# A two-block transformer stack in split fp32: operand parts side by side in one 512-column matmul, and a convolution's first tap on ScalarE

## The chip, the cores and the metric

The kernel runs on one core of a Trainium2 chip. The metric is the device time of one execution in microseconds (us). A profiled execution gives the trace from which all rows below come.

The engines are named as the profile names them: PE (TensorE, matmuls; PEld its weight loads), DVE (VectorE), ACT (ScalarE), POOL (GpSimd), SP (issues the DMAs).

## The reference, cut to what matters

256 tokens of 2048 channels pass through two blocks. The first has two layers; each is a mixer and a gated convolution feed-forward ("ffn"), with RMS norms before and after. The second has two "hybrid" layers that mix four kinds of attention. Nearly all arithmetic is projections `h @ w` of 256 tokens with big fp32 weight matrices. The ffn, where the second edit lies:

```python
def causal_dwconv(x, w, b):          # K = 3 taps
    xp = jnp.pad(x, ((0, 0), (K - 1, 0), (0, 0)))
    y = xp[:, 0:T] * w[0]
    for k in range(1, K):
        y = y + xp[:, k:k + T] * w[k]
    return y + b

def channel_mixer(h, up, conv_w, conv_b, down):
    hid = causal_dwconv(h @ up, conv_w, conv_b)
    gate, val = jnp.split(hid, 2, axis=-1)
    return (jax.nn.gelu(gate, approximate=True) * val) @ down
```

## The kernel before, in words

**Layout.** Activations lie transposed: 128 channels on the partitions, 256 tokens along the free axis, so a "column tile" of a projection is 128 output channels and its result is 128 x 256 in PSUM. A k tile is 128 input channels.

**Split products.** PE multiplies in a rounded form of fp32 (float32r). Each operand is therefore kept as a rounded part and the rest that rounding left: weights as `h` and `l` (L147 on ACT rounds, L148 on DVE subtracts, 128 x 1024 at a time), activations as `xh` and `xl` (`split`, L206 and L207; in class `XS` with the norm's gain, L277 and L278). A product is h·xh + l·xh + h·xl, three matmuls of 256 columns into the same PSUM range: L173, L174 and L177 (L180 where more than two columns are open at once, for then the third products follow together). The two parts of activations lie in separate tiles of eight k tiles each.

**Weight stream.** 899 blocks of 512 KB come by DMA on SP's queue into 5 raw buffers and are split into 4 buffers each of `h` and `l`; 8 weight tiles of 128 x 128 per block, in the order in which the program asks for them.

**projT** computes some columns over all k tiles, then evacuates them with `evac` (a callback). Two columns share a PSUM bank (`pts[ci // 2][:, ci % 2]`), out of the pool `pp` of 4 banks. With `hold` the evacuation is handed back as a function, and `hooks` calls such functions in the middle of the next projection: each stage starts with a held group of five or six columns, then a group with hooks, in which the norm's factor is computed. `projV` (L198 to L200) is the same with tokens and channels exchanged: weights are the moving operand, 512 columns at a time. `out_proj` runs six columns together (none in the ffn), then pairs up to column 13, then columns 14 and 15 singly, for the norm that follows at once. The attention's own products use a second PSUM pool, `pa`, of 4 banks.

**Around it.** In the ffn, `unit(j, ps)` takes a pair of columns (gate and value), multiplies with the norm's factor (L532, the reader of PSUM), applies the three taps (L537, then two L540 for each half), gelu (L543, ACT), the product (L544) and `split`. In the projections of queries and keys the evacuation is `ev_mul` (L395); out_proj's are `Post.evac` (L313 square on ACT, L319 on DVE) and, in the hybrid layers, L1103. In the hybrid layers gated linear attention comes first: six levels of decays (L902 to L907), products (L888) and masked copies (L891), then chunk states and a norm (L863 writes its end); after it in the program stand the four column pairs of diff_q and diff_k. The 2 KB tiles `w2` (8 of them) serve all short-lived values, `a8` (13, of 8 KB) the long ones.

**Order.** The program is unrolled. A scheduler orders each engine's instructions ahead of time: of those whose inputs and buffers are ready it takes the one that stands first in the program, moved by the offsets of `tc.high_priority`: new weight blocks 3000 instructions ahead, evacuations `EVAC` = 100 ahead, L888 250 behind. On the chip each engine then works through its list in order.

Of the kernel before, what the change touches and what calls it, by code (L numbers as in the profile page):

```python
# [10 lines left out]
F32 = mybir.dt.float32  # L11
# [4 lines left out]
OP = mybir.AluOpType  # L16
# [49 lines left out]
def kernel(  # L66
# [20 lines left out]
    wk = ctx.enter_context(tc.tile_pool(name="wk", bufs=8))  # L87
# [73 lines left out]
    def projT(ks, cols, key, xs, evac, hooks={}, hold=False):  # L161
        nb = (len(cols) + 1) // 2
        pts = [pp.tile([P, 2, T], F32, tag="pp", name="pp") for _ in range(nb)]
        for i, k in enumerate(ks):
            if i in hooks:
                hooks[i]()
            xh, xl = xs(k)
            last = i == len(ks) - 1
            cs = []
            for ci, c in enumerate(cols):  # L170
                h, l = blk(key(k, c))
                o = pts[ci // 2][:, ci % 2]
                TE.matmul(o, h, xh, start=(i == 0 and ci % 2 == 0), stop=False, skip_group_check=True)  # L173
                TE.matmul(o, l, xh, start=False, stop=False, skip_group_check=True)  # L174
                cs.append((o, h))
                if len(cols) <= 2:
                    TE.matmul(o, h, xl, start=False, stop=last, skip_group_check=True)  # L177
            if len(cols) > 2:
                for o, h in cs:
                    TE.matmul(o, h, xl, start=False, stop=last, skip_group_check=True)  # L180
        def evacs():
            with tc.high_priority(offset=EVAC):
                for b in range(nb):
                    evac(b, pts[b])

        if hold:
            return evacs
        evacs()

    def projV(ks, key, xs, evac):  # L190
        pts = [pp.tile([P, 512], F32, tag="pp", name="pp") for _ in range(2)]
        for i, k in enumerate(ks):
            xh, xl = xs(k)
# [11 lines left out]
    def split(val, hi, lo):  # L205
        S.activation(out=hi, in_=val, func=AF.Copy)  # L206
        V.tensor_tensor(out=lo, in0=val, in1=hi.bitcast(F32), op=OP.subtract)  # L207

# [4 lines left out]
    def rsqrt(ss, n, width):  # L213
        # 1 / sqrt(y), y = ss / width + eps, from p = 2 sqrt(y) of the table and Heron's step: p / 4y + 1 / p
# [52 lines left out]
    class XS:  # L267
        def __init__(self, gname):
            self.g = gname
            self.h = [a8(F32R) for _ in range(2)]  # L270
            self.l = [a8(F32R) for _ in range(2)]
            self.acc = w2()

        def add(self, k, n=2):
            for j in range(k, k + n):
                hi, lo = self.h[j // 8][:, j % 8], self.l[j // 8][:, j % 8]
                S.activation(out=hi, in_=x_t[:, j], func=AF.Copy, scale=pc(self.g, j))  # L277
                V.scalar_tensor_tensor(out=lo, in0=x_t[:, j], scalar=pc(self.g, j), in1=hi.bitcast(F32),  # L278
                                       op0=OP.mult, op1=OP.subtract)
# [8 lines left out]
        def hooks(self, held):  # L288
            # the norm's short products go between those of the second projection, `held` is the first one's end
# [8 lines left out]
        def __call__(self, k):  # L298
            return self.h[k // 8][:, k % 8], self.l[k // 8][:, k % 8]
# [73 lines left out]
    def pipeline(n, first, second, depth=2):  # L373
        # the second half of each item's work trails its first half by `depth` items
# [24 lines left out]
    def mixer0(xs, post):  # L399
# [76 lines left out]
        ph, pl = a8(F32R), a8(F32R)  # L476
        fo = CST["fix"][0]
        for g in range(4):
# [16 lines left out]
            split(po, ph[:, 2 * g : 2 * g + 2], pl[:, 2 * g : 2 * g + 2])  # L495

        mh, ml = [a8(F32R) for _ in range(2)], [a8(F32R) for _ in range(2)]
# [7 lines left out]
        for g in range(4):  # L505
            def ev_pool(b, ps, g=g):
                t = w2()
                for j in range(2):
                    V.tensor_scalar(out=t[:, j], in0=ps[:, j], scalar1=pc("pool_b", 2 * g + j),
                                    scalar2=pc("pool_s", 2 * g + j), op0=OP.add, op1=OP.mult)  # L510
                split(t, mh[1][:, 2 * g : 2 * g + 2], ml[1][:, 2 * g : 2 * g + 2])
            projT(range(2), [0, 1], lambda k, c, g=g: ("pool_w", 0, g * 256 + k * P, ((c * P, P),)),
                  lambda k, g=g: (ph[:, 2 * g + k], pl[:, 2 * g + k]), ev_pool)

        for h in range(0, 8, 2):
            o = pa.tile([P, 2, T], F32, tag="pa", name="pa")
            for j in range(2):
# [3 lines left out]
            split(o, mh[0][:, h : h + 2], ml[0][:, h : h + 2])  # L521
        sqrt_ready(ml[0][:, 7, 0:1].bitcast(F32))
        out_proj(lambda k, c: ("ab_w_out", 0, k * P, ((c * P, P),)), list(range(8, 16)) + list(range(8)),
                 lambda k: (mh[k // 8][:, k % 8], ml[k // 8][:, k % 8]), post.evac, mid=post.mid)

# [1 line left out]
    def ffn(l, xs, post):  # L527
        fh, fl = [a8(F32R) for _ in range(4)], [a8(F32R) for _ in range(4)]

        def unit(j, ps):  # L530
# [14 lines left out]
            split(g[:, 1], fh[j // 8][:, j % 8], fl[j // 8][:, j % 8])  # L545
# [6 lines left out]
        sqrt_ready(fl[3][:, 7, 0:1].bitcast(F32))  # L552
        kd = lambda k, c: ("ffn_down", l, k * P, ((c * P, P),))
        out_proj(kd, range(32), lambda k: (fh[k // 8][:, k % 8], fl[k // 8][:, k % 8]), post.evac, wide=0, mid=post.mid)

# [1 line left out]
    def mixer1(xs, post):  # L557
# [7 lines left out]
        xch, xcl = a8(F32R), a8(F32R)  # L565
# [5 lines left out]
        def rec_conv(j):  # L571
# [5 lines left out]
            split(xc[:, j : j + 2], xch[:, j : j + 2], xcl[:, j : j + 2])  # L577
# [9 lines left out]
        ch, cl = a8(F32R), a8(F32R)  # L587
        for i in range(6):
            g = pc("qng", i) if i < 4 else pc("kvg", i - 4)
            S.activation(out=ch[:, i], in_=z[:, i], func=AF.Copy, scale=g)  # L590
            V.scalar_tensor_tensor(out=cl[:, i], in0=z[:, i], scalar=g, in1=ch[:, i].bitcast(F32),
                                   op0=OP.mult, op1=OP.subtract)
# [5 lines left out]
        # rotary tables  # L598
# [30 lines left out]
        # recurrence gates  # L629
        gr, gi = a8(), a8()  # L630

        def rec_gate(n):
            def ev_g(b, ps):
# [3 lines left out]
                  lambda k: (xch[:, k], xcl[:, k]), ev_g)  # L637
# [3 lines left out]
        # latent projections  # L641
        xq = lambda k: (ch[:, k], cl[:, k])
        xk = lambda k: (ch[:, 4 + k], cl[:, 4 + k])
# [29 lines left out]
        # softplus(-lambda), with log1p(e) = 2 atanh(e / (2 + e))  # L673
# [18 lines left out]
        mh, ml = [a8(F32R), None], [a8(F32R), None]  # L692
# [13 lines left out]
        def values(hh, p):  # L706
# [5 lines left out]
            if hh % 2:  # L712
                split(ob[0], mh[0][:, hh - 1 : hh + 1], ml[0][:, hh - 1 : hh + 1])
# [3 lines left out]
        # output gate  # L717
# [12 lines left out]
        # recurrence  # L730
        mh[1], ml[1] = a8(F32R), a8(F32R)
# [22 lines left out]
        for j in range(0, 8, 2):  # L754
# [3 lines left out]
            split(t, mh[1][:, e], ml[1][:, e])  # L758
        sqrt_ready(ml[1][:, 7, 0:1].bitcast(F32))
        out_proj(lambda k, c: ("cd_w_out", 0, k * P, ((c * P, P),)), list(range(16)), lambda k: (mh[k // 8][:, k % 8], ml[k // 8][:, k % 8]), post.evac,  # L760
                 mid=post.mid)

# [1 line left out]
    def hybrid(l, xs, consts, nxt, mid=None):  # L764
# [14 lines left out]
        # gla q, k, decay and forget-gate logits  # L779
# [25 lines left out]
        # decay logits of gla, forget gates  # L805
# [12 lines left out]
        # log sigmoid  # L818
# [27 lines left out]
        def norm_trans(ob, n2, g, dst):  # L846
            # ob: psum [P tokens, 2 heads, 2 tiles, 128]; dst: [P, 2 heads, T]
# [17 lines left out]
        # ---- gated linear attention  # L865
# [28 lines left out]
        # A level takes the pairs that its halves part, with decays from the first half's last token, and the  # L894
        # diagonal at that token; the diagonal of a chunk's last token rides in a column that the last level spares.
# [20 lines left out]
        # chunk states  # L916
# [48 lines left out]
        # ---- differential attention  # L965
# [65 lines left out]
        # ---- output gates: K tiles fox 0-3, diff 4-7, moba 8-11, gla 12-15  # L1031
        mh, ml = [a8(F32R) for _ in range(2)], [a8(F32R) for _ in range(2)]

        def gate(nm, j):
# [3 lines left out]
            def ev_gate(b, ps):  # L1038
# [6 lines left out]
                split(t, mh[k0 // 8][:, e], ml[k0 // 8][:, e])  # L1045
# [3 lines left out]
        # ---- forgetting and block attention  # L1049
# [56 lines left out]
        sqrt_ready(ml[1][:, 7, 0:1].bitcast(F32))  # L1106
        out_proj(ko, list(range(8)) + list(range(12, 16)) + list(range(8, 12)), lambda k: (mh[k // 8][:, k % 8], ml[k // 8][:, k % 8]), ev_out, mid=mid)

# [210 lines left out]
```

## Time and profile before

| | |
|---|---|
| time, median of 3 runs (lowest to highest) | 2792.28 us (2791.45 to 2794.66) |
| the profiled execution: span from the first to the last instruction | 2789.4 us |
| PE busy | 2754.7 us, 99% |
| DVE busy | 1864.3 us, 67% |
| ACT busy | 1301.3 us, 47% |
| DMA, mean | 174 GB/s, 484.05 MB |
| mean granted PE clock | 0.993 |

A profiled execution lists no time of its own beside its span; the median of the runs is 2.9 us above it. "Busy" is the time in which an engine has at least one instruction under way. Matmuls are pipelined: the length shown of one is longer than the step from its start to the next one's start, so a busy PE says that it doesn't wait, and the step says what a matmul costs.

### The profile page before, as it was taken

How to read it: one execution, taken by the hardware profiler on the slowest of the kernel's cores; microseconds unless marked ns; L12 is line 12 of the kernel's file. 1: busy time of each engine (PE TensorE's matmuls, PEld its weight loads, DVE VectorE, ACT ScalarE, POOL GpSimd, SP SyncE). 2: the span in 40 equal slices, each digit the busy share in tenths (PEclk: the TensorE clock that was granted, in tenths of full speed). 3: DMA queues.
4: the chain of work that ended last, by engine and by line, in shares of the span. 5: the costliest groups of instructions: out<-in, count | busy, mean ns of one | idle time of the engine just before them, and what ended most of it. 6: DMA issues, size and time to landing. Idle time of an engine off the chain costs nothing.

```text
span 2789.4 us, 52130 instructions
## 1 busy us (share of the span) xinstructions
PE 2754.7 (99%) x21738; PEld 2676.3 (96%) x21738; DVE 1864.3 (67%) x2965; ACT 1301.3 (47%) x1749; POOL 5.8 (0%) x10
## 2 busy tenths in 40 slices
PE   9999999999999999999999999999999999999998
PEld 9998999999999998999999999998889999888998
DVE  6776578777644787678777754676756566675655
ACT  5444454444433475454444443454535444453543
POOL 0000000000000000000000000000000000000000
PEclk9999999999999999999999999999999999999999
DMA  7445545555555454545555555554444555444453
GB/s 253 167 159 175 186 156 185 184 182 183 184 186 182 159 173 132 185 159 182 182 183 184 184 183 181 179 177 157 159 155 167 182 182 175 150 158 156 167 182 129
DMA packets 133324, 484.05 MB, mean 174 GB/s; under 512 B 15136, under 2 KB 16224, under 8 KB 132576
## 3 DMA queue, kind: packets, MB, share of 16 engines
q1 hardware_dynamic: 133088, 480.73, 49.8%
q8 instruction: 170, 2.79, 0.4%
q14 instruction: 66, 0.54, 0.1%
HBM read 476.73 MB, written 2.10 MB: 172 GB/s over the span
## 4 chain that ended last, share of the span: by engine, by line
PE 98%; DVE 1%; ACT 0%; issue 0%; DMA 0%; DVEq 0%; ACTq 0%; SPq 0%
PE pp L173 28%; PE pp L174 28%; PE pp L177 24%; PE pp L180 4%; PE pp L200 3%; PE pp L199 3%; PE pp L198 3%; PE pa L386 1%; PE pa L390 1%; PE pn L240 0%; PE pa L1071 0%; PE pa L888 0%; PE pa L1002 0%; PE pn L254 0%; PE pa L1074 0%
## 5 line engine op out<-in xcount | busy, mean ns | idle before, releaser
L173 PE MATMUL pp<-a,h 128*128 128x256 f32 x6528 | 1826.6, 285 | 12.3 <-ACT a L277 6.9
L174 PE MATMUL pp<-a,l 128*128 128x256 f32 x6528 | 1824.5, 284 | 0.0
L148 DVE TENSOR_TENSOR l<-raw,h 128x1024 fp32r<-128x1024 f32 (+1 forms) x900 | 1100.0, 1223 | 804.7 <-ACT h L147 803.6
L177 PE MATMUL pp<-a,h 128*128 128x256 f32 x5600 | 1588.1, 284 | 0.0
L147 ACT ACTIVATE h<-raw 128x1024 fp32r<-128x1024 f32 (+1 forms) x900 | 950.8, 1057 | 1201.3 <-PE pp L177 837.9
L173 PEld LDWEIGHTS pp<-a,h 128*128 128x128 f32 x6528 | 1258.8, 193 | 15.8 <-ACT a L277 7.7
L174 PEld LDWEIGHTS pp<-a,l 128*128 128x128 f32 x6528 | 1258.5, 193 | 2.6 <-issue 0.7
L177 PEld LDWEIGHTS pp<-a,h 128*128 128x128 f32 x5600 | 1074.6, 192 | 2.8 <-issue 1.7
L180 PE MATMUL pp<-a,h 128*128 128x256 f32 x928 | 140.8, 287 | 0.0
L199 PE MATMUL pp<-l,a 128*128 128x512 f32 x328 | 128.3, 391 | 0.0
L198 PE MATMUL pp<-h,a 128*128 128x512 f32 x328 | 128.3, 391 | 0.0
L200 PE MATMUL pp<-h,a 128*128 128x512 f32 x328 | 128.3, 391 | 0.0
L180 PEld LDWEIGHTS pp<-a,h 128*128 128x128 f32 x928 | 126.3, 197 | 0.0
L540 DVE SCALAR_TENSOR_TENSOR w<-w,prm_t,w 128x254 f32<-128x254 f32 (+1 forms) x256 | 116.6, 479 | 2.0
L200 PEld LDWEIGHTS pp<-h,a 128*128 128x128 f32 x328 | 61.6, 188 | 13.4 <-issue 0.7
L199 PEld LDWEIGHTS pp<-l,a 128*128 128x128 f32 x328 | 61.6, 188 | 12.5
L198 PEld LDWEIGHTS pp<-h,a 128*128 128x128 f32 x328 | 61.8, 188 | 12.2
L543 ACT ACTIVATE w<-w 128x256 f32<-128x256 f32 x64 | 26.6, 416 | 89.1 <-DVE w L540 89.1
L364 ACT ACTIVATE w<-w,s 128x128 f32<-128x128 f32 x96 | 42.9, 447 | 52.6 <-DVE s L360 52.6
L206 ACT ACTIVATE a<-w 128x256 fp32r<-128x256 f32 (+1 forms) x92 | 43.7, 477 | 11.5 <-DVE w L544 3.0
L537 DVE TENSOR_SCALAR w<-w,prm_t 128x256 f32<-128x256 f32 x128 | 47.2, 410 | 2.0
L207 DVE TENSOR_TENSOR a<-w,a 128x256 fp32r<-128x256 f32 (+1 forms) x92 | 45.8, 500 | 1.4 <-ACT a L206 1.4
(247 smaller groups left out, 1297.5 us busy)
## 6 DMA issues: line engine op xcount, KB each, us to landing
raw<-in_wpk_dram SPq DMA_DIRECT2D x898, 512.0 KB, 3.3
a<-in_cst_dram SPq DMA_DIRECT2D x2, 1024.0 KB, 5.6
x_t<-in_xT_dram SPq DMA_DIRECT2D x1, 1024.0 KB, 11.2
a<-a SPq DMA_DIRECT2D x8, 128.0 KB, 4.9
out_dram<-a SPq DMA_DIRECT2D x2, 512.0 KB, 2.7
x_t<-in_xT_dram SPq DMA_DIRECT2D x1, 640.0 KB
a<-a SPq DMA_DIRECT2D x8, 64.0 KB
out_dram<-a SPq DMA_DIRECT2D x2, 256.0 KB
```

Source lines behind the costliest of these rows:

```text
L147: S.activation(out=h[:, a], in_=r[:, a], func=AF.Copy)
L148: V.tensor_tensor(out=l[:, a], in0=r[:, a], in1=h[:, a].bitcast(F32), op=OP.subtract)
L173: TE.matmul(o, h, xh, start=(i == 0 and ci % 2 == 0), stop=False, skip_group_check=True)
L174: TE.matmul(o, l, xh, start=False, stop=False, skip_group_check=True)
L177: TE.matmul(o, h, xl, start=False, stop=last, skip_group_check=True)
L180: TE.matmul(o, h, xl, start=False, stop=last, skip_group_check=True)
L198: TE.matmul(pts[q], xh[:, sl], h, start=(i == 0), stop=False, skip_group_check=True)
L199: TE.matmul(pts[q], xh[:, sl], l, start=False, stop=False, skip_group_check=True)
L200: TE.matmul(pts[q], xl[:, sl], h, start=False, stop=last, skip_group_check=True)
L207: V.tensor_tensor(out=lo, in0=val, in1=hi.bitcast(F32), op=OP.subtract)
L537: V.tensor_scalar(out=y[:, s], in0=hp[:, s], scalar1=wc(2), scalar2=pc(f"fcb{l}", c), op0=OP.mult, op1=OP.add)
L540: V.scalar_tensor_tensor(out=y[:, s, d:], in0=hp[:, s, : T - d], scalar=wc(k), in1=y[:, s, d:], op0=OP.mult, op1=OP.add)
```

## The change: what it does

- Activations' two parts lie side by side, in tiles `[P, 4, 2, T]` (class `HL`; four k tiles a tile, k tile by k tile first the rounded part, then the rest). The number of `a8` tiles stays.
- In `projT`, a group is *wide* when it has more than four k tiles, at most two columns, and neither `hold` nor `hooks`; in `out_proj` the pairs are wide and columns 14 and 15 are not. A wide group gives each column a PSUM bank of its own. One matmul takes h times both parts (512 columns, the whole bank), a second l times the rounded part (256 columns, the bank's first half).
- At a wide group's end `summed` adds the halves: per column an ACT copy of the second half to SBUF and a DVE add of the first half to it. `evac` then gets the sum in SBUF in place of PSUM.
- The ffn's first tap (scale and bias) moves from DVE to ACT (`Identity`).
- `w2` has 10 tiles in place of 8. Everything else of the diff puts the new class where the pairs of tiles were; comments go.

```diff
-    wk = ctx.enter_context(tc.tile_pool(name="wk", bufs=8))
+    wk = ctx.enter_context(tc.tile_pool(name="wk", bufs=10))
-    def projT(ks, cols, key, xs, evac, hooks={}, hold=False):
-        nb = (len(cols) + 1) // 2
-        pts = [pp.tile([P, 2, T], F32, tag="pp", name="pp") for _ in range(nb)]
+    def projT(ks, cols, key, xs, evac, hooks={}, hold=False, wide=None):
+        n = len(cols)
+        if wide is None:
+            wide = len(ks) > 4 and n <= 2 and not hold and not hooks
+        pts = [pp.tile([P, 2, T], F32, tag="pp", name="pp") for _ in range(n if wide else (n + 1) // 2)]
...
                 h, l = blk(key(k, c))
+                if wide:
+                    TE.matmul(pts[ci], h, x, start=first, stop=False, skip_group_check=True)
+                    TE.matmul(pts[ci][:, 0], l, x[:, 0], start=False, stop=last, skip_group_check=True)
+                    continue
...
+        def summed():
+            rest, u = w2(), w2()
+            for j in range(n):
+                S.activation(out=rest[:, j], in_=pts[j][:, 1], func=AF.Copy)
+                V.tensor_tensor(out=u[:, j], in0=pts[j][:, 0], in1=rest[:, j], op=OP.add)
+            return u
+
         def evacs():
             with tc.high_priority(offset=EVAC):
-                for b in range(nb):
-                    evac(b, pts[b])
+                if wide:
+                    evac(0, summed())
+                else:
+                    for b in range((n + 1) // 2):
+                        evac(b, pts[b])
...
+    class HL:
+        def __init__(self, n):
+            self.t = [a8(F32R, [P, 4, 2, T]) for _ in range((n + 3) // 4)]
+        def part(self, s, k, n):
+            assert k % 4 + n <= 4
+            return self.t[k // 4][:, k % 4 : k % 4 + n, s]
+        def split(self, val, k, n):
+            hi, lo = self.part(0, k, n), self.part(1, k, n)
+            S.activation(out=hi, in_=val, func=AF.Copy)
+            V.tensor_tensor(out=lo, in0=val, in1=hi.bitcast(F32), op=OP.subtract)
...
+        def __call__(self, k):
+            return self.t[k // 4][:, k % 4]
...
             projT(korder, [c, c + 1] if c < 14 else [c], key, xs, lambda b, ps, c=c: evac(c, ps),
-                  {len(korder) // 2: mid} if mid and c == 15 else {})
+                  {len(korder) // 2: mid} if mid and c == 15 else {}, wide=c < 14)
...
-                V.tensor_scalar(out=y[:, s], in0=hp[:, s], scalar1=wc(2), scalar2=pc(f"fcb{l}", c),
-                                op0=OP.mult, op1=OP.add)
+                S.activation(out=y[:, s], in_=hp[:, s], func=AF.Identity, scale=wc(2), bias=pc(f"fcb{l}", c))
```

## Rows read from the trace of the kernel before

**Rows 1.** The profile's page: span, busy time of PE, its chain by engine.
```profile
span 2789.4 us, 52130 instructions
...
PE 2754.7 (99%) x21738; PEld 2676.3 (96%) x21738; DVE 1864.3 (67%) x2965; ACT 1301.3 (47%) x1749; POOL 5.8 (0%) x10
...
PE 98%; DVE 1%; ACT 0%; issue 0%; DMA 0%; DVEq 0%; ACTq 0%; SPq 0%
```

**Rows 2.** Groups by line: count, busy us, mean ns, idle before and its releasers.
```profile
L177 PE MATMUL pp<-a,h 128*128 128x256 f32 x5600 | 1588.1, 284 | 0.0
...
L180 PE MATMUL pp<-a,h 128*128 128x256 f32 x928 | 140.8, 287 | 0.0
```

**Rows 3.** Timeline of PE, steady stretch: start us, length us, instruction.
```profile
1000.00 0.28 PE L173 MATMUL pp<-a,h 128*128 128x256 f32 x1
...
1005.88 0.28 PE L174 MATMUL pp<-a,l 128*128 128x256 f32 x1
```

**Rows 4.** Timeline of PE in projV.
```profile
239.66 0.39 PE L200 MATMUL pp<-h,a 128*128 128x512 f32 x1
...
242.83 0.39 PE L199 MATMUL pp<-l,a 128*128 128x512 f32 x1
```

**Rows 5.** Windows: length, busy us of PE, PEld, DVE, ACT, POOL; clock, DMA.
```profile
418.50:729.50 311.00, 311.00 (x2594) 311.00 (x2593) 237.90 (x373) 137.14 (x169) 0.00 (x0) 1.00 0.53 183
...
741.10:902.00 160.90, 160.90 (x1344) 160.90 (x1343) 79.90 (x82) 64.88 (x66) 0.00 (x0) 1.00 0.54 183
...
360.00:385.00 25.00, 21.29 (x157) 20.73 (x156) 19.31 (x40) 11.02 (x19) 0.00 (x0) 0.86 0.33 116
```

**Rows 6.** Waits: who waited for whom, us in total, times, longest.
```profile
ACT h L147 <- PE pp L177: 837.9, 512, 4.2
```

**Rows 7.** Groups by line and shape, for ACT and DVE.
```profile
L537 DVE TENSOR_SCALAR w<-w,prm_t 128x256 f32<-128x256 f32 x128 | 47.2, 410 | 2.0
...
L319 DVE TENSOR_SCALAR a<-pp,prm_t 128x256 f32<-128x256 f32 x64 | 30.1, 478 | 0.0
...
L573 ACT ACTIVATE a<-a,prm_t 128x256 f32<-128x256 f32 x8 | 4.4, 589 | 0.0
L634 ACT ACTIVATE a<-pp,prm_t 128x256 f32<-128x256 f32 x8 | 3.8, 477 | 0.0
```

**Rows 8.** Timelines of DVE and PE at the first ffn's start.
```profile
419.60 0.68 DVE L532 TENSOR_TENSOR w<-pp,rb 128x512 f32<-128x512 f32 x1
...
431.25 0.68 DVE L532 TENSOR_TENSOR w<-pp,rb 128x512 f32<-128x512 f32 x1
...
418.51 0.28 PE L173 MATMUL pp<-a,h 128*128 128x256 f32 x1
```

**Rows 9.** Timelines of PE and DVE behind out_proj's six columns.
```profile
305.15 0.28 PE L173 MATMUL pp<-a,h 128*128 128x256 f32 x1
...
307.10 1.27 DVE L319 TENSOR_SCALAR a<-pp,prm_t 128x256 f32<-128x256 f32 x3
...
2226.34 1.29 DVE L1103 TENSOR_TENSOR x_t<-x_t,pp 128x512 f32<-128x512 f32 x2 [1.52 <-PE pp L180]
```

**Rows 10.** Timeline of DVE in the first hybrid layer's gated linear attention.
```profile
1889.13 1.36 DVE L891 COPY_PREDICATED a<-a,pa 128x512 f32<-128x512 uint8 x2
...
1910.08 0.68 DVE L395 TENSOR_TENSOR a<-pp,rb 128x512 f32<-128x512 f32 x1
...
1923.94 0.68 DVE L395 TENSOR_TENSOR a<-pp,rb 128x512 f32<-128x512 f32 x1
```

**Rows 11.** Timeline of PE there.
```profile
1858.00 0.28 PE L173 MATMUL pp<-a,h 128*128 128x256 f32 x1
...
1872.74 1.16 PE L888 MATMUL pa<-w,w 64*128 64x128 f32 x14
```

**Rows 12.** Windows of that stretch, pp's instructions alone, then all.
```profile
1869.40:1910.00 40.60, 25.84 (x189) 23.25 (x188) 0.00 (x0) 0.00 (x0) 1.00 0.32 115
...
1869.40:1910.00 40.60, 39.87 (x357) 35.55 (x356) 30.70 (x58) 14.28 (x29) 0.00 (x0) 1.00 0.32 115
```

More of the change, by code (lines that the diff above doesn't have):

```diff
@@ L166, in projT @@
                 hooks[i]()
-            xh, xl = xs(k)
-            last = i == len(ks) - 1
+            x = xs(k)
+            first, last = i == 0, i == len(ks) - 1
             cs = []
@@ L203, in projV, with scaled, end @@
                 evac(q, pts[q])
-    def split(val, hi, lo):
-        S.activation(out=hi, in_=val, func=AF.Copy)
-        V.tensor_tensor(out=lo, in0=val, in1=hi.bitcast(F32), op=OP.subtract)
+    class HL:
[8 more added lines that the diff above has]
+            V.tensor_tensor(out=lo, in0=val, in1=hi.bitcast(F32), op=OP.subtract)
+        def scaled(self, val, g, k):
+            hi, lo = self.part(0, k, 1)[:, 0], self.part(1, k, 1)[:, 0]
+            S.activation(out=hi, in_=val, func=AF.Copy, scale=g)
+            V.scalar_tensor_tensor(out=lo, in0=val, scalar=g, in1=hi.bitcast(F32), op0=OP.mult, op1=OP.subtract)
+        def end(self, k):
+            return self.part(1, k, 1)[:, 0, 0:1].bitcast(F32)
+        def __call__(self, k):
+            return self.t[k // 4][:, k % 4]
     eps_t = cp.tile([P, 1], F32, name="eps_t")
@@ L269, in __init__ @@
             self.g = gname
-            self.h = [a8(F32R) for _ in range(2)]
-            self.l = [a8(F32R) for _ in range(2)]
+            self.x = HL(KT)
             self.acc = w2()
@@ L275, in add @@
             for j in range(k, k + n):
[L276 to L279, printed above, removed]
+                self.x.scaled(x_t[:, j], pc(self.g, j), j)
         def squares(self):
@@ L494, in mixer0 @@
                                        op0=OP.mult, op1=OP.subtract)
-            split(po, ph[:, 2 * g : 2 * g + 2], pl[:, 2 * g : 2 * g + 2])
-        mh, ml = [a8(F32R) for _ in range(2)], [a8(F32R) for _ in range(2)]
+            po_x.split(po, 2 * g, 2)
+        mx = HL(16)
         vt = a8(shape=[P, 2, 1024])
@@ L520, in mixer0 @@
                      o[:, j], j == 0)
-            split(o, mh[0][:, h : h + 2], ml[0][:, h : h + 2])
-        sqrt_ready(ml[0][:, 7, 0:1].bitcast(F32))
+            mx.split(o, h, 2)
+        sqrt_ready(mx.end(7))
         out_proj(lambda k, c: ("ab_w_out", 0, k * P, ((c * P, P),)), list(range(8, 16)) + list(range(8)),
-                 lambda k: (mh[k // 8][:, k % 8], ml[k // 8][:, k % 8]), post.evac, mid=post.mid)
+                 mx, post.evac, mid=post.mid)
     def ffn(l, xs, post):
-        fh, fl = [a8(F32R) for _ in range(4)], [a8(F32R) for _ in range(4)]
+        fx = HL(32)
         def unit(j, ps):
@@ L551, in ffn @@
             projT(range(KT), gc(j, 1), key, xs, lambda b, ps, j=j: unit(j, ps), xs.hooks(held) if j == 3 else {})
-        sqrt_ready(fl[3][:, 7, 0:1].bitcast(F32))
+        sqrt_ready(fx.end(31))
         kd = lambda k, c: ("ffn_down", l, k * P, ((c * P, P),))
-        out_proj(kd, range(32), lambda k: (fh[k // 8][:, k % 8], fl[k // 8][:, k % 8]), post.evac, wide=0, mid=post.mid)
+        out_proj(kd, range(32), fx, post.evac, wide=0, mid=post.mid)
     def mixer1(xs, post):
@@ L586, in mixer1 @@
         _, rqb = rstd_sb([sqs[i][:, j] for i in range(2) for j in range(2)], 512)
-        ch, cl = a8(F32R), a8(F32R)
+        cx = HL(6)
         for i in range(6):
[L589 to L592, printed above, removed]
+            cx.scaled(z[:, i], pc("qng", i) if i < 4 else pc("kvg", i - 4), i)
         rec_input(2)
@@ L757, in mixer1 @@
             V.tensor_tensor(out=t, in0=gy[:, e], in1=xc[:, e], op=OP.mult)
-            split(t, mh[1][:, e], ml[1][:, e])
-        sqrt_ready(ml[1][:, 7, 0:1].bitcast(F32))
-        out_proj(lambda k, c: ("cd_w_out", 0, k * P, ((c * P, P),)), list(range(16)), lambda k: (mh[k // 8][:, k % 8], ml[k // 8][:, k % 8]), post.evac,
+            mr.split(t, j, 2)
+        sqrt_ready(mr.end(7))
+        out_proj(lambda k, c: ("cd_w_out", 0, k * P, ((c * P, P),)), list(range(16)), lambda k: mx(k) if k < 8 else mr(k - 8), post.evac,
                  mid=post.mid)
@@ L1029, in hybrid @@
         pipeline(4, dscores, dvalues, depth=1)
-        mh, ml = [a8(F32R) for _ in range(2)], [a8(F32R) for _ in range(2)]
+        mx = HL(16)
         def gate(nm, j):
@@ L1104, in ev_out @@
             nxt(c, n)
-        sqrt_ready(ml[1][:, 7, 0:1].bitcast(F32))
-        out_proj(ko, list(range(8)) + list(range(12, 16)) + list(range(8, 12)), lambda k: (mh[k // 8][:, k % 8], ml[k // 8][:, k % 8]), ev_out, mid=mid)
+        sqrt_ready(mx.end(15))
+        out_proj(ko, list(range(8)) + list(range(12, 16)) + list(range(8, 12)), mx, ev_out, mid=mid)
     def dump():
```

43 lines of the change are left out of this document (22 added, 21 removed).

## The prediction, made before the changed kernel was run

> **What bounds the kernel now.** I read the page's busy shares and its chain first [rows 1]: TensorE is busy 2754.7 of 2789.4 us and holds 98% of the chain, so only what changes TensorE's stream, or makes it wait, moves the time. Then the groups by line [rows 2]: the weight-by-operand products are single 256-column matmuls, three for each pair of one k tile and one column tile (I call such a pair a unit): weight part h times operand part h, weight l times operand h, weight h times operand l. L177 is the third product where at most two columns run side by side (5600 units), L180 the third where five or six do (928). Then TensorE's timeline in the steady part [rows 3]: a matmul starts every 0.120 us (49 of them from 1000.00 to 1005.88), although each is shown as 0.28 us long, so the start-to-start step is the price and a unit costs 0.360 us. The same kernel has 512-column matmuls in projV, each with its own weight load as well [rows 4]: 14 steps from 239.66 to 242.83, which is 0.2264 us each. The granted clock is 1.00 in the steady stretches [rows 5], the 2.4 GHz level. Going from 256 to 512 columns costs 0.1064 us, which is 256 columns at 2.4 GHz (0.1067); so of the 0.120 us some 0.0135 us are spent per matmul whatever its width. That is what the change can win, once per unit.
>
> Around TensorE there is room: in the 311 us of the first ffn's up projection DVE is busy 237.9 and ACT 137.1, in its down projection 79.9 and 64.9 of 160.9 [rows 5]. The weight splits run ahead: what ends ACT's longest wait is TensorE giving back weight tiles (837.9 us in 512 waits) [rows 6].
>
> **The change, part by part.**
>
> *The gain.* A wide unit is one 512-column matmul (h times both operand parts) and one of 256 (l times the rounded part): 0.2264 + 0.120 = 0.3464 us in place of 0.360, 0.0136 us less. By the code, wide is every projT with more than four k tiles, one or two columns, no hold and no hooks, and in out_proj every pair before column 14. Counted: layer 0's mixer 528 units, the two ffns 1344 each (28 up pairs of 32 units, 7 down pairs of 64), layer 1's mixer 368, the two hybrid layers 736 each; 5056 in all. They fit L177's 5600 less 192 (with hooks), 96 (one, two or four k tiles) and 256 (columns 14 and 15) [rows 2]. Gain: 5056 x 0.0136 = 68.6 us. Bounds: with the step of 512 columns taken as 0.227 it is 65.7 us; I see no row by which it would be more than 69.
>
> The Trainium skill ("TensorE: Matmul & The Clock Gate", Back-to-back issue gap) speaks against this: it gives the isolated gap as columns over 2.4 GHz plus only 2.5 ns. By that rule a unit would win 2.5 ns, 12.6 us in all. The trace's 0.120 and 0.2264 us do not agree with it.
>
> *What the column's end costs.* 145 wide groups have 288 columns. Each column gets an ACT copy of 256 columns out of PSUM (0.477 us, the nearest row is L634) and a DVE add with one PSUM operand (0.478, L319) [rows 7]; the operation that follows then reads SBUF and not PSUM. That is 137 us more on ACT and 138 on DVE over the kernel. The 128 first taps leave DVE (0.410 each, L537: 52 us) and join ACT (0.589 by the convolution that is there already, L573: 75 us) [rows 7]. In the up projection a unit pair of 11.5 us had 237.9 x 11.52 / 311 = 8.8 us of DVE and 5.1 of ACT [rows 5]; afterwards it lasts 11.1 us with 8.8 + 0.96 - 0.82 = 8.9 and 5.1 + 0.95 + 1.18 = 7.2. Both stay below 11.1, so I price this at nothing; the cover is TensorE's next group. The cover fails if DVE takes 25% longer than that (11.1 / 8.9); each us beyond is then paid in each of the 54 wide pairs of the two up projections. A hand-over between ACT and DVE is added in both places; that is latency of one or two us and not load.
>
> *What is late next: PSUM.* pp has four banks. A group used one, and now uses two, so TensorE may be one group ahead of the evacuation and no longer three. In the steady part that is enough: 11.1 us to do copy, add, copy, add. It is not where an evacuation comes late. I looked for these places:
>
> (a) Ffn start. The six held columns fill three banks, the hooked group the fourth; the next group takes its second column into the bank that L532 reads at 419.60 to 420.28, and would want it at 418.51 + 0.35 [rows 8]. 1.4 us, twice: 3 us (0 to 8, if the fourth bank, read at 431.25, is missed as well).
>
> (b) out_proj's first pair after the six columns. It starts at 305.15, its second column 0.35 later; the first bank of the six is read until two L319 of the three that start at 307.10 are done, 307.95 [rows 9]. 2.4 us in each of two mixers: 5 us. The hybrid layers free that bank with one add of 0.65 us (L1103 [rows 9]): nothing. Where a wide pair stands ahead of the six columns (three places), the third bank is late by some 0.7 us: 2 us.
>
> (c) Gated linear attention in the hybrid layers. The first pair of diff_q is done at 1869.5 (96 matmuls from 1858.00), and its evacuation runs at 1910.08, the first of four L395 for the four pairs; two more follow within 3 us, the last at 1923.94 [rows 10, 11]. Until then three groups sit in PSUM, one bank each, and TensorE works on: 189 of its 357 matmuls between 1869.4 and 1910.0 are for pp [rows 12], 22.7 us at 0.120, so 17.9 us are the attention's. With two banks a group, the third pair can't begin until the first pair's sums are read. That three run at once suggests that they stood for their common output tile and not for DVE; no row says it. The new sums go into w2 tiles, so they can go earlier; but they need two of ten w2 tiles, which the six levels take first. The levels give tiles back as their masked copies are done; the fifth is at 1889.13 [rows 10]. TensorE would be through the second pair at about 1883 (1858.0 + 2 x 11.1 + three levels of 1.2 us [rows 11]): 7 us idle in each layer, 14 in all. Bounds: 0, if the tiles come at once; 25 a layer, if the sums wait for the end of the phase (40.6 - 11.1 - 17.9 = 11.6, and up to 11 for levels that are put behind the second pair, and some more).
>
> Sum: 2789.4 - 68.6 + 3 + 5 + 2 + 14 = 2744.8 us of span. The three runs' median of 2792.28 is 2.9 above the span, so 2748 us. The norm chains and both last columns keep their form, so nothing is taken off there.
>
> **The rivals.**
>
> *Nothing is late.* The list of ready work puts the sums in between, and only 5 us of (a) to (c) are left: 2726 + 2.9 = 2729. For it: DVE has idle time in the phase of (c), 30.7 of 40.6 us busy [rows 12]. Against it: the levels are earlier in the program.
>
> *The sums wait until the attention's end.* 20 us a layer and 10 elsewhere: 2789.4 - 68.6 + 50 + 2.9 = 2774. For it: the evacuations of before ran at the phase's end.
>
> *Slower: PSUM shuts TensorE out.* One mechanism, at (c): if the first pair's banks are held until the last of the evacuations of before (1923.94 [rows 10]), TensorE idles 1923.9 - 1869.5 - 11.1 - 17.9 = 25.4 us, 8 more as the levels' matmuls start behind the second pair, and the clock falls as it does behind a norm, where a stretch of 25 us has 0.86, 3.5 us lost [rows 5]: 37 us a layer. 74 + 10 - 68.6 = +15: 2808. It decides from 29 us a layer. Against it: the sums don't need what the evacuations waited for.
>
> *A cost in each group.* If the weight splits, in order behind copies that wait for a group's end, come late by 0.45 us in every wide group, 65 us go and the time stays at 2790. Against it: weights are four tiles ahead, and ACT waits for TensorE, not the other way [rows 6].
>
> *The 0.0135 us are not per matmul* but come with each 256 columns of an operand tile: a unit stays at 0.360, nothing is won, and with the 24 lost it is 2789.4 + 24 + 2.9 = 2816. The two timelines speak against it [rows 3, 4]. The Trainium skill's rule above is the milder form of it: 12.6 us won would leave 2804.
>
> *The change doesn't do what it says* can't be here: which groups are wide follows from their arguments.
>
> **How the numbers follow.** Forecast (2737 to 2762) 0.55; nothing late 0.13; sums at the phase's end 0.17; shut out 0.07; a cost in each group 0.06; fixed cost not per matmul 0.02. From 2728 to 2782 are 0.83 of it. A measurement of this kernel tells 0.2% (5.6 us) from no change. Faster: the first three and some of the group cost, 0.87; same 0.04; slower 0.09.
>
> **What would show it.** TensorE's timeline in the up projection has steps of 0.226 and 0.120 in turn, 11.1 us a pair: otherwise the gain falls. The 512-column group of projT has 5056 matmuls. DVE's share there stays near 80%, ACT's near 65%, without table loads at each tap. TensorE's waits name the new copy or add, above all 1880 to 1920 us from the start and the like half a thousand later; if they add up to over 30 us, (c) was too cheap, and if they are under 6, too dear. The prediction is wrong if the steady pairs take over 11.2 us, or if a phase that isn't listed waits over 10 us.

## The result, and the profile after

The changed kernel takes 2818.64 us (median of 4 runs, 2810.94 to 2825.84) against 2791.86 (2791.03 to 2794.66) in the runs of the kernel before beside it: ratio 1.0092, 95% interval 1.0066 to 1.0118. The forecast of 2748 was wrong, in sign too. The four runs stand in two places, 2811 (twice) and 2826 (twice); the profiled one is of the first. Its page, which answers to [rows 1]:

```profile
span 2809.2 us, 42670 instructions
...
PE 2728.4 (97%) x16682; PEld 2419.7 (86%) x16682; DVE 1919.1 (68%) x3125; ACT 1465.1 (52%) x2165; POOL 5.8 (0%) x10
...
PEclk9999999999999999999999999979899998889999
```

TensorE has 5056 matmuls fewer and 26 us less busy time, but the span grew by 20. Its granted clock (the line of 40 slices, in tenths of full speed) falls in a few slices, where the kernel before had 9 throughout. To see where the time goes, I took from both traces the start of each projection group on TensorE. The table has before's start and, for each other kernel, how much earlier (-) or later the same group starts. The last four columns are experiments told of below: "narrow d" is run 1, "own" run 3, "order" run 9, "own+order" run 8.

```
first matmul of                before   after  narrow d    own   order  own+order
first ffn, first wide pair      418.5    -6.4     -5.1    -5.6    -5.4     -5.4
first ffn, down projection      741.1   -18.3    -11.0   -11.6   -15.5    -15.5
layer 1's mixer                 931.4   -24.2    -13.5   -14.5   -20.3    -20.3
second ffn, first wide pair    1277.7   -25.8    -14.2   -17.8   -23.3    -24.0
second ffn, down projection    1600.3   -31.7    -20.2   -23.7   -33.4    -34.2
hybrid 0, diff_q/k pair 0      1858.0   -35.9    -23.6   -27.9   -38.5    -40.7
hybrid 0, diff_v               1922.9   -14.5    -23.4   -27.6   -17.9    -40.7
hybrid 0, fox_q pair 2         1944.7   -14.5    -23.4   -27.5   -18.0    -40.6
hybrid 0, moba_q pair 0        2012.7    -2.0     -9.7   -29.4    -6.0    -42.7
hybrid 1, diff_q/k pair 0      2348.9    -7.8    -14.7   -34.5   -11.5    -48.2
hybrid 1, diff_v               2413.9    13.5    -14.4   -34.1     9.4    -48.1
hybrid 1, moba_q pair 0        2503.6    26.0     -2.1   -36.0    21.5    -50.1
last column                    2769.3    20.3     -7.0   -39.5    16.0    -55.3
```

The gain comes, 35.9 us up to the hybrid layers. Each hybrid layer then loses at two places and no other: 21.4 us between the first diff pair and diff_v, 12.5 between fox_q pair 2 and moba_q.

TensorE's timeline in the first ffn (start, length) answers to [rows 3]: the starts are 0.230 and 0.117 us apart, 0.347 a unit.

```profile
599.75 0.39 PE L177 MATMUL pp<-a,h 128*128 128x512 f32 x1
599.98 0.28 PE L178 MATMUL pp<-a,l 128*128 128x256 f32 x1
600.10 0.39 PE L177 MATMUL pp<-a,h 128*128 128x512 f32 x1
600.33 0.28 PE L178 MATMUL pp<-a,l 128*128 128x256 f32 x1
600.45 0.39 PE L177 MATMUL pp<-a,h 128*128 128x512 f32 x1
```

In the second ffn the same instructions run in another pattern, which repeats every three units:

```profile
1400.01 0.40 PE L177 MATMUL pp<-a,h 128*128 128x512 f32 x1
1400.25 0.28 PE L178 MATMUL pp<-a,l 128*128 128x256 f32 x1
1400.36 0.40 PE L177 MATMUL pp<-a,h 128*128 128x512 f32 x1
...
1400.71 0.40 PE L177 MATMUL pp<-a,h 128*128 128x512 f32 x1
...
1401.07 0.40 PE L177 MATMUL pp<-a,h 128*128 128x512 f32 x1
```

From 1400.01 to 1401.07 are three units, so 0.353 us each; this ffn keeps it to the end of its down projection, and the first ffn keeps 0.347. Below, 0.353 is called the slower pattern. The windows (columns as in [rows 5]: length, busy us of PE, PEld, DVE, ACT, POOL, clock, DMA) show both at full clock, and the two stretches that lose:

```profile
411.00:711.00 300.00, 300.00 (x1735) 264.57 (x1735) 237.80 (x368) 183.32 (x280) 0.00 (x0) 1.00 0.57 190
...
1251.90:1568.50 316.60, 316.60 (x1794) 274.37 (x1793) 245.66 (x379) 188.84 (x290) 0.00 (x0) 1.00 0.57 186
...
1848.40:1883.80 35.40, 20.07 (x142) 15.50 (x140) 20.52 (x57) 9.04 (x29) 0.00 (x0) 0.59 0.06 19
1969.40:1986.30 16.90, 9.24 (x35) 5.77 (x33) 9.35 (x37) 8.89 (x27) 0.00 (x0) 0.64 0.12 42
```

At 1848.4 the second diff pair is done; the third starts at 1883.81. In between TensorE has only the attention's 142 matmuls, is idle for 15 us, and runs at a granted clock of 0.59. Timelines of that end, ACT first:

```profile
1869.31 0.28 ACT L886 ACTIVATE w<-pa 128x128 f32<-128x128 f32 x1 [9.48 <-PE pa L994]
...
1878.32 0.28 ACT L886 ACTIVATE w<-pa 128x128 f32<-128x128 f32 x1 [6.26 <-PE pa L994]
...
1879.50 0.30 ACT L260 ACTIVATE nr<-s,eps_t 128x4 f32<-128x4 f32 x1
1879.71 0.91 ACT L193 ACTIVATE w<-pp 128x256 f32<-128x256 f32 x3
```

```profile
1883.34 1.08 DVE L194 TENSOR_TENSOR w<-pp,w 128x256 f32<-128x256 f32 x3
1884.33 0.68 DVE L433 TENSOR_TENSOR a<-w,rb 128x512 f32<-128x512 f32 x1
```

```profile
1880.79 1.25 PE L896 MATMUL pa<-cst_t,w 128*128 128x128 f32 x4 [2.50 <-DVE w L891]
1883.81 0.80 PE L177 MATMUL pp<-a,h 128*128 128x512 f32 x1 [1.76 <-DVE w L194]
```

The copies (L193) of the first pair, whose last matmul started at 1833.33, run 46 us later, right behind the squares (L886) and the root (L260) of the attention's second norm, although ACT stood idle for 9.48 and 6.26 us before. The second place has the same shape: the last matmul of fox_k pair 4 starts at 1954.51, its copies come at 1984.72 behind the norm of the differential attention, and fox_v starts at 1986.30.

```profile
1982.05 0.28 ACT L886 ACTIVATE w<-pa 128x128 f32<-128x128 f32 x1 [4.84 <-PE pa L1058]
...
1984.72 1.19 ACT L193 ACTIVATE w<-pp 128x256 f32<-128x256 f32 x4
```

### The profile page after: what moved, and what is told of

Same layout as the page of the kernel before. It is cut to its first block, busy times and chain, and to the rows that moved or that the text cites. A ratio compares the mean times of both kernels' runs of the same rounds, so it can differ in the third digit from the quotient of the medians.

```text
span 2809.2 us, 42670 instructions
## 1 busy us (share of the span) xinstructions
PE 2728.4 (97%) x16682; PEld 2419.7 (86%) x16682; DVE 1919.1 (68%) x3125; ACT 1465.1 (52%) x2165; POOL 5.8 (0%) x10
## 4 chain that ended last, share of the span: by engine, by line
PE 61%; DVE 2%; ACT 1%; issue 0%; DVEq 0%; ACTq 0%
PE pp L177 25%; PE pp L178 13%; PE pp L181 4%; PE pp L182 4%; PE pp L188 2%; PE pp L218 2%; PE pp L220 2%; PE pp L219 2%; PE pp L185 1%; PE pa L424 0%; PE pa L1105 0%; PE pa L428 0%; DVE a L925 0%; PE pa L896 0%; ACT L260 0%
## 5 line engine op out<-in xcount | busy, mean ns | idle before, releaser
L177 PE MATMUL pp<-a,h 128*128 128x512 f32 x5056 | 1777.6, 396 | 3.5 <-DVE w L194 3.5
L177 PEld LDWEIGHTS pp<-a,h 128*128 128x128 f32 x5056 | 949.9, 188 | 223.3 <-DVE w L194 4.1
L178 PEld LDWEIGHTS pp<-a,l 128*128 128x128 f32 x5056 | 957.7, 189 | 2.7 <-issue 1.0
L181 PE MATMUL pp<-a,h 128*128 128x256 f32 x1472 | 392.2, 288 | 15.2 <-ACT a L242 6.9
L181 PEld LDWEIGHTS pp<-a,h 128*128 128x128 f32 x1472 | 287.3, 195 | 17.3 <-ACT a L242 7.8
L182 PEld LDWEIGHTS pp<-a,l 128*128 128x128 f32 x1472 | 287.2, 195 | 0.6 <-DVE l L148 0.4
L185 PE MATMUL pp<-a,h 128*128 128x256 f32 x544 | 153.9, 283 | 0.0
L188 PE MATMUL pp<-a,h 128*128 128x256 f32 x928 | 140.6, 286 | 0.0
L188 PEld LDWEIGHTS pp<-a,h 128*128 128x128 f32 x928 | 125.8, 196 | 0.0
L193 ACT ACTIVATE w<-pp 128x256 f32<-128x256 f32 x288 | 104.0, 385 | 12.1 <-PE pp L178 0.5
L194 DVE TENSOR_TENSOR w<-pp,w 128x256 f32<-128x256 f32 x288 | 108.4, 417 | 0.0
L577 DVE SCALAR_TENSOR_TENSOR w<-w,prm_t,w 128x255 f32<-128x255 f32 (+1 forms) x256 | 107.4, 479 | 0.2
L185 PEld LDWEIGHTS pp<-a,h 128*128 128x128 f32 x544 | 104.2, 192 | 0.0
L220 PEld LDWEIGHTS pp<-h,a 128*128 128x128 f32 x328 | 62.6, 191 | 13.9 <-issue 1.1
```

Of the source, the lines that this page charges most:

```text
L177: TE.matmul(pts[ci], h, x, start=first, stop=False, skip_group_check=True)
L178: TE.matmul(pts[ci][:, 0], l, x[:, 0], start=False, stop=last, skip_group_check=True)
L181: TE.matmul(o, h, x[:, 0], start=(first and ci % 2 == 0), stop=False, skip_group_check=True)
L182: TE.matmul(o, l, x[:, 0], start=False, stop=False, skip_group_check=True)
L185: TE.matmul(o, h, x[:, 1], start=False, stop=last, skip_group_check=True)
L188: TE.matmul(o, h, x[:, 1], start=False, stop=last, skip_group_check=True)
```

## The experiments

The theory: (1) two unsummed wide groups fill the four banks and shut TensorE out; (2) the sums come late because their buffers are taken from the common ring of work tiles, which are given out in program order, and the norms' tiles are earlier in the program. Rivals: the wide groups' ends load ACT and DVE everywhere; two banks a group are too few whenever the sums come; the sums' priority; the ring's length; the tap. All ratios are to the kernel before, with 95% intervals. A gap is the time from the start of a pair's last matmul to the start of the next projection's first.

**1. Narrow diff pairs.**

```diff
-                      lambda b, ps, o=4 * i + j: ev_mul(dq, xs)(o // 2, ps))
+                      lambda b, ps, o=4 * i + j: ev_mul(dq, xs)(o // 2, ps), wide=False)
```

> Only the four diff_q/diff_k pairs of each hybrid layer go back to three 256-column matmuls in one bank; all else as in the changed kernel. Theory A (two late-summed groups fill the four banks, the third pair shuts TensorE out): from the start of the first pair to the start of diff_v the stretch goes back from 86.3 to about 65 us a layer, so about 2 x 21 us less and some 2 us of lost gain: 2771 us (2785 where the run falls with the upper of the two clusters of the changed kernel, 2811 and 2825). The second place (fox_k 6 to fox_v, 12 us a layer) stays. Theory B (the ends of the wide pairs load ScalarE and VectorE everywhere, the stall at the third pair is only where it shows): the time stays at 2811 to 2825, the stall moves to diff_v.

Measured: 2784.57 us, 0.9976 (0.9966 to 0.9985). The first place is gone (-23.6 to -23.4 in the table), the second stays (13.7 and 12.3 us), with the clock down in it again:

```profile
1960.50:1978.70 18.20, 10.80 (x34) 6.62 (x32) 9.32 (x37) 8.84 (x26) 0.00 (x0) 0.56 0.12 38
```

Part (1) holds, and the two places are separate. The time is the upper of the two expected: this run's first ffn has the slower pattern too (5.9 us won in the up projection, not 11.9).

**2. Narrow diff and fox pairs**, the same argument in the fox pairs as well.

> The diff_q/diff_k pairs and the fox_q/fox_k pairs (and no others) go back to three 256-column matmuls. Theory A: both stalls go (21.4 and 12.4 us a layer, 67.6 us in all), and about 4 us of gain with them: 2748 us, faster than the kernel before by 1.5%. Theory B: not below 2790, since the wide pairs elsewhere cost what they gain.

Measured: 2756.92 us, 0.9876 (0.9861 to 0.9891). Both places are gone (the offset goes from -23.4 to -23.2 over them in the first hybrid layer). The wide groups elsewhere do pay, against the first rival; the 9 us over the expectation are again the slower pattern, in both ffns.

**3. Own buffers for the sums**, all pairs wide.

```diff
-    wk = ctx.enter_context(tc.tile_pool(name="wk", bufs=10))
+    wk = ctx.enter_context(tc.tile_pool(name="wk", bufs=8))
-            rest, u = w2(), w2()
+            u = wk.tile([P, 2, T], F32, tag="sum", name="sum", bufs=2)
-                S.activation(out=rest[:, j], in_=pts[j][:, 1], func=AF.Copy)
-                V.tensor_tensor(out=u[:, j], in0=pts[j][:, 0], in1=rest[:, j], op=OP.add)
+                S.activation(out=u[:, j], in_=pts[j][:, 1], func=AF.Copy)
+                V.tensor_tensor(out=u[:, j], in0=pts[j][:, 0], in1=u[:, j], op=OP.add)
```

> All pairs stay wide. The sums of a column's end get two buffers of their own, written in place (copy of the second half into it, the sum over the copy), and the common buffers go from 10 back to 8: the same memory. Theory A1 (the sums come late because their buffer comes from the common ring, behind the norm of the gated linear attention in program order): they now come right behind their pair, the stretch of the four pairs is about 60 us a layer and the one of the fox pairs about 65, both stalls go: 2744 us (2740 to 2755). Theory A2 (two banks a pair are too few beside that attention, whenever the sums come): the third pair still waits, 2790 to 2825.

Measured: 2754.34 us, 0.9866 (0.9851 to 0.9881). ACT's timeline has the copies right behind their pairs (whose last matmuls start at 1841.27 and 1856.35), ahead of the levels' exponentials (L938), and the stretch from there to the fourth pair's end has the full clock:

```profile
1841.23 0.73 ACT L193 ACTIVATE sum<-pp 128x256 f32<-128x256 f32 x2
...
1856.32 0.73 ACT L193 ACTIVATE sum<-pp 128x256 f32<-128x256 f32 x2 [2.01 <-PE pp L178]
...
1858.92 0.61 ACT L938 ACTIVATE w<-w 128x512 f32<-128x512 f32 x1
```

```profile
1856.40:1892.80 36.40, 35.76 (x265) 29.15 (x264) 29.23 (x63) 16.42 (x35) 0.00 (x0) 1.00 0.35 120
```

With the same banks and the same memory both losses are gone, so two banks a group are enough. The run changes two things, the ring and the number of tiles a group; run 10 parts them.

**4. Higher priority of the sums** (the changed kernel with `tc.high_priority(offset=2000 if wide else EVAC)`).

> The changed kernel with the scheduler's priority of the sums raised to 2000. If their low priority were what makes them late: both stalls go, 2744 us. Theory A1 (they have no buffer, whatever their priority): they still stand behind the squares of the norm of the attention's second half, 2811 or 2825 us as the changed kernel.

Measured: 2824.3 us, 1.0118 (1.0103 to 1.0133). The gap before the third pair is 32.8 us in the first hybrid layer and 35.6 in the second. The priority isn't it.

**5. A longer ring** (the changed kernel with `wk` at 12, the weights' staging ring at 4).

> The changed kernel with the common ring of work buffers at twelve, not ten (the staging ring of the weights at four, not five, to have the memory). Theory A1 (a buffer of the common ring comes in program order, so more of them don't let the sums past the norm): both stalls stay, 2811 to 2826 us. Rival (the ring was only too short): the stalls go, 2745 to 2765 us.

Measured: 2819.12 us, 1.0103 (1.0086 to 1.012). The gaps are 34.0 and 17.5 us in the first hybrid layer. Two more tiles change nothing; longer rings were not run.

**6. Six banks** (`pp` 6, `pa` 2).

> The changed kernel with six banks for projections and two, not four, for the attention's products. The sums still come late. Theory A (the third pair waits because two unsummed pairs hold all four banks): the third pair of diff_q/diff_k now has banks and starts by 1860, the stretch of the four pairs is shorter by 5 to 20 us a layer (the fourth pair waits in its place); the attention's own steps, with half of their banks, may lose some of it. Rival (TensorE is shut out by the order of its instructions or by something else than banks): the third pair still starts some 35 us after the second ended.

Measured: 2787.9 us, 0.9987 (0.9977 to 0.9996). The third pair starts with a gap of 0.1 us (at 1864.3, as all of this kernel is some 15 us later than the changed one there), the fourth waits in its place, 17 us; diff pair 0 to diff_v is 78.3 us, not 86.3. Part (1) again; fewer banks for the attention cost elsewhere (the first ffn starts 8 us later), and that part I did not follow up.

**7. No wide group**, the layout, ring and tap kept (`wide = False`).

> No group is wide: three 256-column matmuls as before, with the change's other parts kept (part and rest side by side, ten work buffers, first tap on ScalarE). Theory A (these parts cost and give nothing): 2790 to 2794 us, as the kernel before. Rival (the tap on ScalarE or the side-by-side layout carries a part of the result): more than 5 us off 2792, and the step of 120 ns in the gated feed-forward changes.

Measured: 2792.59 us, 1.0001 (0.9992 to 1.0011); no group of the table starts more than 1.4 us off before's. Together those parts neither cost nor give.

**8. The order within a row**, on top of 3: both 512-column matmuls of a k tile, then both of 256.

```diff
                 if wide:
                     TE.matmul(pts[ci], h, x, start=first, stop=False, skip_group_check=True)
-                    TE.matmul(pts[ci][:, 0], l, x[:, 0], start=False, stop=last, skip_group_check=True)
+                    cs.append((pts[ci][:, 0], l))
                     continue
...
+            if wide:
+                for o, l in cs:
+                    TE.matmul(o, l, x[:, 0], start=False, stop=last, skip_group_check=True)
```

> The kernel with the sums in buffers of their own, with the matmuls of a row of a pair in another order: 512, 512, 256, 256 columns and no longer 512, 256, 512, 256. It asks whether the two patterns seen (0.347 and 0.353 us for a 512 and a 256 together, each held for a whole stage) hang on the alternation. Theory P (it is the alternation of long and short): one pattern throughout, 0.346 to 0.348 us, some 9 us a feed-forward less where the slower one stood: 2735 to 2742 us. Theory Q (two patterns are there in any order, or come from somewhere else): stages at about 0.353 stay, 2748 to 2758 us.

Measured: 2735.99 us, 0.9801 (0.9786 to 0.9815), the best of all, and its four runs lie within 0.36 us, where 3 had 5.3. Its page and a timeline of the second ffn:

```profile
span 2734.1 us, 42675 instructions
...
PE 2694.5 (99%) x16682; PEld 2386.1 (87%) x16682; DVE 1913.6 (70%) x3125; ACT 1452.4 (53%) x2165; POOL 5.8 (0%) x10
```

```profile
1399.62 0.62 PE L177 MATMUL pp<-a,h 128*128 128x512 f32 x2
1400.08 0.40 PE L188 MATMUL pp<-a,l 128*128 128x256 f32 x2
...
1401.01 0.62 PE L177 MATMUL pp<-a,h 128*128 128x512 f32 x2
```

Four units in 1.39 us, 0.348 each; from the third pair on every pair of both up projections takes 11.15 us (10.1 us won in the first, 10.2 in the second). That lies between the two patterns of the alternating order, near the better one, and there is only one.

**9. The order alone**, on the changed kernel.

> The changed kernel (sums still in the common ring of ten) with only the order of a row's matmuls changed to 512, 512, 256, 256 columns. Theory A with P (two losses that add up: late sums 67.6 us, the slower pattern of the alternating order some 9 us a feed-forward): the stalls before the third diff pair and before fox_v stay at about 34 and 17 us, the two clusters (2811, 2825) become one, near 2736 + 67 = 2803 us. Rival (the order also lets the sums come earlier, and the gain with the sums' own buffers was partly that): below 2790 us.

Measured: 2807.08 us, 1.0056 (1.0041 to 1.0071), four runs within 1.4 us. The two stretches stand as they were:

```profile
1845.50:1881.10 35.60, 20.83 (x144) 16.36 (x142) 20.62 (x57) 8.87 (x28) 0.00 (x0) 0.57 0.06 19
1965.70:1982.70 17.00, 9.73 (x35) 6.19 (x34) 9.26 (x37) 8.76 (x25) 0.00 (x0) 0.62 0.10 34
```

So the order doesn't move the sums; the own buffers are worth 2807.08 - 2735.99 = 71 us with it. The spread of the changed kernel went with the alternating order.

**10. In place, in the common ring**: 3 and the order together, but the sums' tile from the ring of ten again (`u = w2()`). It parts the two things that 3 changed at once.

> The kernel with the sums written in place and the order 512, 512, 256, 256, but their one tile taken from the common ring again (ten tiles, as in the changed kernel). It separates the two things that the kernel with own buffers changed at once: a tile less for each group, and a ring of its own. Theory A1 (the ring's program order): both gaps stay, 34 to 36 and 17 us, 2805 to 2808 us, as with the order alone. Rival (two tiles a group were one too many for the ring): the gaps go, 2736 us.

Measured: 2805.79 us, 1.0054 (1.0037 to 1.007). The gaps are 32.8 and 16.7 us in the first hybrid layer, 35.4 and 16.8 in the second. One tile less a group does nothing; the ring of its own does it all, 2805.79 - 2735.99 = 70 us. In the changed kernel and in runs 4, 5, 6, 9 and 10, all with the common ring, the first pair's copies start 0.2 us behind the start of the second norm's root. That the sums' place in the ring decides is shown; that the ring gives its tiles out in program order fits these places, but no run changed the program's order.

**11 and 12. The first tap back on VectorE**, on 3 and on 8.

> The kernel with the sums in buffers of their own, with the first tap back on VectorE. Each pair of the gated feed-forward takes TensorE 11.1 to 11.3 us; VectorE then has 16 more of its instructions' time in every pair it can hide. Theory A (VectorE is covered either way): 2750 to 2758 us, as with the tap on ScalarE. Rival (with the sums of the columns VectorE is now near full there, and the tap on ScalarE is what makes room): the pairs of the feed-forward lengthen beyond 11.3 us, 56 pairs by some tenths, 2765 us or more.

> The kernel with own buffers for the sums and the order 512, 512, 256, 256, with the first tap back on VectorE. Without the two patterns the part of the tap is to be seen alone. Theory A (off the path on either engine): 2735 to 2737 us, no difference that can be measured. Rival (the tap on ScalarE makes room on VectorE at the ends of the feed-forwards and in the pairs): 2739 us or more; the other way (ScalarE is the later of the two): 2733 or less.

Measured: 2747.69 us on 3 (four runs from 2735.13 to 2752.24, below both expectations and too wide to tell anything so small) and 2735.49 on 8 (2735.05 to 2737.51, against 2735.76 to 2736.12): no difference. This edit is free and worth nothing here.

## Why the prediction was wrong

*The gain per unit* was right where the pattern is 0.347 (0.0133 us won, forecast 0.0136) and half of it where it is 0.353 (0.0067). The first ffn's up projection won 11.9 us, the second's 5.9; over the second ffn (1344 units) and some pairs of layer 1's mixer and the hybrid layers that is some 11 us of the 68.6. The prediction had taken one step for each width and no interplay of the two, and the second ffn's pairs at 11.31 us are over the 11.2 that it had named as a sign of being wrong. That in the runs near 2826 the first ffn has the slower pattern as well is likely (runs 1 to 6 all show it there) but not shown, since the profiled run is one of the others. The Trainium skill ("TensorE: Matmul & The Clock Gate", Back-to-back issue gap) gives the isolated gap as columns over 2.4 GHz plus 2.5 ns; by it, as an estimate, 2.5 ns a unit could be won. Neither pattern agrees with it (13.3 and 6.7 ns won).

*The ends of the columns* were free as forecast: DVE is busy 79% and ACT 61% in the first ffn's up projection (237.80 and 183.32 of 300), against 80% and 65%. (The 54 wide pairs that the prediction counts there are 56, 28 in each; nothing hangs on it.)

*(a) and (b)* were priced too dear, 10 us for about 2.5 by the starts of the groups (1.7 in layer 1's mixer, 0.2 in each hybrid layer, the rest in tenths). At the first ffn's start DVE's read runs from 411.87 to 412.56, and TensorE works on through it: two 512-column matmuls start at 412.48 and 412.71, the second column's first among them, and the pair takes 11.17 us, not 11.09. Behind layer 0's six columns the program's order runs the pair's first column alone for eight k tiles, until the second bank is free. Its end is seen where two 512-column matmuls follow each other:

```profile
303.34 0.28 PE L178 MATMUL pp<-a,l 128*128 128x256 f32 x1
303.46 0.64 PE L177 MATMUL pp<-a,h 128*128 128x512 f32 x2
```

Only the six columns behind a wide pair in layer 1's mixer wait (1.48 us for L194).

*(c) is the step that failed*, with its sentence "The levels give tiles back as their masked copies are done". TensorE was through the second pair when the prediction said (1848.4 + 35.9 = 1884 in before's time, forecast 1883). But the sums did not follow the fifth level; their copies followed the second norm's root, 24 us later (1855.85 here, 1879.71 in the rows above):

```profile
1855.85 1.32 DVE L925 COPY_PREDICATED a<-a,pa 128x512 f32<-128x512 uint8 x2
```

So TensorE went 35.4 us without a projection where the prediction had 7 us idle. The argument against the slower rival, that the sums don't need what the evacuations waited for [rows 10], was true and not enough. In run 3 the sums (L194) of both pairs are done while the evacuation into the common output tile (L433) still waits for the end of the first norm (L897), as it did before:

```profile
1858.05 0.76 DVE L194 TENSOR_TENSOR sum<-pp,sum 128x256 f32<-128x256 f32 x2
...
1890.22 0.75 DVE L897 TENSOR_SCALAR a<-pa,prm_t 128x512 f32<-128x512 f32 x1 [1.70 <-PE pa L896]
1890.89 0.68 DVE L433 TENSOR_TENSOR a<-sum,rb 128x512 f32<-128x512 f32 x1
```

What the prediction missed is that the sums' own tiles, in the common ring, stand behind the norms' tiles and so come as late for a reason of their own. Runs 3, 4, 5 and 10 show it: only tiles outside that ring move the sums.

The prediction's sign for (c) would have misled: it asked for TensorE's waits for the new add, with under 6 us meaning "too dear". TensorE's list of waits has only 3.5 us there for L194. The longest wait of that list stands at the attention's own instructions, which TensorE does while it is shut out of the projections; it was not in before's list (us in total, times, longest):

```profile
PE pa L896 <- DVE w L891: 24.7, 8, 3.8
```

*A place was not listed*: fox_k to fox_v, the same mechanism behind the differential attention's norm. Its gap of 16.9 us is the prediction's other sign of being wrong, an unlisted phase that waits over 10 us.

*Sum*: counting the gain inside the stretches (1.7 and 1.3 us at 0.0136 a unit), the first place cost 21.4 + 1.7 = 23 us a layer where 7 stood, the second 12.5 + 1.3 = 14 where nothing stood: 2 x 16 + 2 x 14 = 60 us; 11 from the slower pattern; 7.5 less from (a) and (b). That is 63.5 of the 64.4 us between the forecast span of 2744.8 and the 2809.2 measured. Of the rivals, "the sums wait until the attention's end" had the mechanism and nearly the size at the first place: 20 us a layer, (c)'s upper bound 25, measured 23. It had no second place. "PSUM shuts TensorE out" had 37 us a layer, all at one place; that 23 + 14 at two places make 37 as well is luck, and with it that its 2808 lies near 2811.

*The clock* belongs to the loss but did not start it: with the sums early the same attention work runs at 1.00 (run 3). As an estimate, it can hold at most half of the 20.07 us of TensorE's work in the first stretch, 10 us, if all of that work ran at the 1.2 GHz level; how much of it lies on the path I did not separate.

## What to carry to other kernels

A change that doubles what a unit holds (PSUM banks here) must be checked wherever its release comes late, and the release is only as early as the buffer that it writes to: give short-lived sums buffers of their own, not places in a ring shared with long phases. Before trusting that an engine with idle time will do an instruction early, look for what it needs besides the engine. A single step per instruction width, read where all instructions are alike, is not yet a price for a mix of widths; here the order within the mix was worth 18 us (2754.34 - 2735.99) with the sums' own buffers, and 12 without (2818.64 - 2807.08).

## What the hardware showed that I had not expected

The alternating stream of 512 and 256 columns has two steady patterns at full granted clock, 0.347 us a unit and one of period three at 0.353 (steps of 0.235, 0.114, 0.232, 0.118, 0.241 and 0.120 us in turn). From its third pair on, each ffn keeps one of them to the end of its down projection. Of the 16 ffns in the eight profiled runs with the alternating order, only the changed kernel's first has 0.347. Two long and two short in turn gave 0.348 in both ffns. What makes a stage begin in one or the other stays open, and so does whether all of the 0.0133 us could be had for good. And where TensorE was left with 20 us of work in 35, the granted clock fell to 0.59 of full speed, so a part of the stretch was at the 1.2 GHz level and a part at 2.4, while 25 us with 21.3 busy had 0.86 [rows 5].
